# Making the Hyena filters of both layers at the start of a two-layer backbone

## The chip, the cores and the metric

The kernel runs on one core of a Trainium2 chip. The metric is the device time of one execution in microseconds (us), the median of three runs. The engines are named as the profile names them: PE (matrix products), PEld (its weight loads), DVE (vector), ACT (scalar functions), POOL (GpSimd) and SP (which issues most transfers).

## The reference, cut to what matters

Two layers work on 1,024 latent tokens and 256 context tokens of width 1,024. Each layer normalises and modulates its input by numbers made from the conditioning vectors, sends it through one input projection, and gives the parts to three mixers: latent attention, a chunkwise mLSTM and a Hyena convolution. An output projection and a convolutional FFN follow. The Hyena convolution needs a filter that depends on the layer's weights and on the position alone, not on the data:

```python
def hyena_filter(seq, w1, b1, w2, b2, w3, sin_freq):
    ...
    hdn = jnp.sin(freq * (z @ w1.astype(f32) + b1.astype(f32)))
    hdn = jnp.sin(freq * (hdn @ w2.astype(f32) + b2.astype(f32)))
    filt = hdn @ w3.astype(f32)
    ...
    h_fwd = filt[:, :HY_WIDTH] * window
    h_bwd = filt[:, HY_WIDTH:] * window
    l1 = jnp.sum(jnp.abs(h_fwd), axis=0) + jnp.sum(jnp.abs(h_bwd[1:]), axis=0)
    ...
    return taps / l1
```

Layer 0 needs it for 1,024 and for 256 positions, layer 1 for 1,024 alone.

## The kernel before, in words

Features lie on partitions and tokens along the free axis, in three blocks: two of 512 latent tokens and one of the 256 context tokens (block 2). Most float32 products are made in three passes on a high and a low part, so that one tile of a projection is many matmuls (`mm`, L252 in the trace), all into the two PSUM banks `pj` and `pk` in turn.

The program begins with the modulation numbers of layer 0 (`ada`): eight steps, each with four weight tiles by DMA, 16 matmul records into a tile `a`, an ACT copy `adarow`, four small matmuls into a tile `a`, and a DVE addition into `mods`. Between them stand the sums of squares for the first norm (`nsq` on ACT, `nacc` on DVE). From the last of these comes the scale `A`; then `norm` makes the hi/lo tiles `B` of each block with one ACT and two DVE operations for each of eight tiles.

`mixers_in` follows, for each layer: the filters, the low-rank queries (`Q0` to `Q2`, with statistics in the bank `ap`), the gate statistics of the mLSTM (`ml_gates`, bank `mm`: transposes of the gates, running sums `mlLF`/`mlLI`, maxima `mlB` and `mlast`, a recurrence `mlmrow` over nine chunks, then `mlRR`, `mldg` and `mlE`), the tiles `U0` and `U1`, the values V and the output gates O (both `by_token`, matmuls `pk<-wh,B` of 128x256), and the products with `wqk` that need the gate statistics' place in the bank `mm`.

`filters` works by blocks of positions: a matmul `f<-zemb,hw`, a `sine`, a matmul `f<-sn_h,hw`, a second `sine`, and then for every 128 positions a matmul `f<-hw,sn_h`, a window product `fb` (DVE), absolute values `fab` (ACT), sums `fl` (POOL), and the sum and difference `ft` (DVE and POOL), which go to DRAM as `taps`. A last small matmul `f<-c_ones,fl` gives the norm `hsc`. A `sine` is seven DVE operations on 64 partitions (one reads the PSUM bank, two find the multiple of two pi in `sn_k`, three subtract it in three parts, one clamps) and one ACT `Sin` into `sn_h`. The blocks follow one another through one buffer each of `sn_a`, `sn_k` and `sn_h`.

Instructions are put on each engine's queue in an order that a scheduler fixes when the program is built: `with self.later(LATER_F)` lets the filters be scheduled as if they had been written 100 instructions later, so that they fill gaps. On the chip each engine then works through its queue in that order.

Of the kernel before, what the change touches and what calls it, by code (L numbers as in the profile page):

```python
# [17 lines left out]
DEPTH = 2  # L18
# [4 lines left out]
TP = 1282                     # token axis with a zero after each stream: x 0:1024, 0, ctx 1025:1281, 0  # L23
# [11 lines left out]
# (first token, columns, stream: 0 latent / 1 context)  # L35
# [16 lines left out]
def _consts():  # L52
# [47 lines left out]
def _host(inp):  # L100
    """Lay the inputs out for the chip: slices, transposes, replication."""
# [4 lines left out]
    def colmaj(a):                       # [L, n*128] -> [L, 128, n]  # L106
        return a.reshape(a.shape[0], -1, 128).transpose(0, 2, 1)
# [52 lines left out]
    qk = np.zeros((L, 2, 2, 128, 128), np.float32)           # [L, pair, q/k, in, out]  # L160
# [9 lines left out]
    o["hyv"] = np.stack([g["hy_b1"], g["hy_b2"], g["hy_sin_freq"]], -1)   # [L,64,3]  # L170
# [19 lines left out]
class Kern:  # L190
# [52 lines left out]
    def later(self, by):  # L243
        """Scheduled as if traced `by` instructions later: work that fills gaps."""
# [9 lines left out]
    def mm3(self, out, lh, ll, rh, rl, start, stop):  # L254
        """One K tile of a float32 product carried by three float32r passes."""
# [4 lines left out]
    def ps(self, shape=(128, 512)):  # L260
        """The next of the two banks that all phases share."""
# [9 lines left out]
    def bpair(self, b):  # L271
        """hi and lo of one block of tokens; the context block carries a zero at each end."""
# [204 lines left out]
    def filters(self, L, sp, pp, tag):  # L477
# [11 lines left out]
        for blk in (range(3) if L < DEPTH - 1 else range(2)):  # L489
# [11 lines left out]
            for i in range(n // 128):  # L501
# [8 lines left out]
                if kk in (0, 8):  # L510
                    nc.vector.memset(fb[0:1, 1], 0.0)
# [1177 lines left out]
```

## Time and profile before

| | |
|---|---|
| median of three runs | 3830.62 us (3816.39 to 3831.75) |
| span of the profiled execution | 3828.4 us |
| PE busy | 3547.6 us, 93% of the span |
| DVE busy | 2001.4 us, 52% |
| ACT busy | 1294.6 us, 34% |
| POOL busy | 923.9 us, 24% |

The profile is one execution. Its span of 3828.4 us is its own time, 2.2 us under the median of the timed runs, and within their spread. "Busy" is the sum of an engine's instructions; a matmul record's end is modelled, so a busy PE is not PE at its peak. In the rows, "idle before" is the time that the engine stood still ahead of an instruction, with the instruction that ended the wait.

### The profile page before, as it was taken

What the parts mean: (1) busy time and instruction counts of PE and PEld (TensorE: products, weight loads), DVE (VectorE), ACT (ScalarE), POOL (GpSimd) and SP (SyncE); (2) the same over time, 40 slices, a digit from 0 to 9 for tenths busy, and PEclk for the clock granted to TensorE, in tenths of its full rate; (3) what the DMA queues carried; (4) which work ended last, traced back from release to release, by engine and by line L of the source; (5) the groups of instructions that cost most, each with busy time, mean ns of one, the idle gap of its engine ahead of it and who ended that gap; (6) DMA issues with size and microseconds to landing.
All of it is one profiled execution on the core that took longest, in us unless ns stands there. A gap on an engine that the chain in (4) does not pass through costs nothing.

```text
span 3828.4 us, 45926 instructions
## 1 busy us (share of the span) xinstructions
PE 3547.6 (93%) x17696; PEld 2809.5 (73%) x17696; DVE 2001.4 (52%) x3037; ACT 1294.6 (34%) x2108; POOL 923.9 (24%) x782
## 2 busy tenths in 40 slices
PE   5999869989899999999999799978999999999997
PEld 3798755556677888888888678856666778888885
DVE  5646675445565433434334765566666543444345
ACT  4433314445543221212112443324566432222222
POOL 1402442222311111111112141143334122222221
PEclk8999989989999999999999899889999999999998
DMA  5322544466242111111111222343232311111111
GB/s 176 115 69 90 198 130 141 126 168 170 71 138 66 39 34 39 39 33 34 39 39 39 94 95 88 108 141 105 54 84 80 102 44 44 45 55 45 44 50 66
DMA packets 195007, 319.46 MB, mean 83 GB/s; under 512 B 32207, under 2 KB 112160, under 8 KB 194788
## 3 DMA queue, kind: packets, MB, share of 16 engines
q1 hardware_dynamic: 194244, 316.23, 26.6%
q8 instruction: 139, 2.28, 0.3%
q14 instruction: 80, 0.66, 0.1%
q0 software_dynamic: 544, 0.31, 0.0%
HBM read 263.50 MB, written 52.81 MB: 83 GB/s over the span
## 4 chain that ended last, share of the span: by engine, by line
PE 59%; DVE 6%; DMA 3%; ACT 2%; issue 2%; POOL 1%; SPq 0%; DVEq 0%; ACTq 0%; POOLq 0%
PE u L252 29%; PE pk L252 12%; PE pj L252 12%; PE st L252 2%; PE pv L252 2%; PE hf L252 1%; ACT wh L300 1%; PE mi L252 0%; DVE B L456 0%; DMA vst<-Ph 0%; PE sm L252 0%; DVE sa L453 0%; PE mo L252 0%; DMA B<-mix 0%; DVE S L1515 0%
## 5 line engine op out<-in xcount | busy, mean ns | idle before, releaser
L252 PE MATMUL u<-B,wh 128*128 128x512 f32 (+1 forms) x3240 | 727.0, 376 | 17.6 <-ACT wh L300 10.6
L252 PEld LDWEIGHTS u<-B,wh 128*128 128x128 f32 x3240 | 573.9, 189 | 141.3 <-ACT wh L300 12.7
L301 POOL TENSOR_TENSOR wh<-wr,wh 128x1024 fp32r<-128x1024 f32 x92 | 222.3, 2416 | 1116.1 <-ACT wh L300 1116.1
L300 ACT CAST wh<-wr 128x1024 fp32r<-128x1024 f32 (+2 forms) x188 | 188.8, 1005 | 775.9 <-PE u L252 425.8
L252 PE MATMUL u<-B,wx 128*128 128x512 f32 (+1 forms) x2040 | 435.1, 367 | 2.3 <-DVE sa L1469 2.3
L252 PEld LDWEIGHTS u<-B,wx 128*128 128x128 f32 x2040 | 352.6, 189 | 70.9 <-issue 2.5
L252 PE MATMUL pj<-B,wh 128*128 128x512 f32 (+1 forms) x1644 | 381.8, 378 | 16.2 <-DVE wh L301 7.0
L252 PE MATMUL pk<-B,wh 128*128 128x512 f32 (+1 forms) x1485 | 355.9, 386 | 31.9 <-ACT S L588 7.8
L252 PEld LDWEIGHTS pj<-B,wh 128*128 128x128 f32 x1644 | 288.5, 193 | 83.6 <-issue 11.9
L252 PEld LDWEIGHTS pk<-B,wh 128*128 128x128 f32 x1485 | 265.7, 197 | 102.2 <-issue 15.3
L1515 DVE SCALAR_TENSOR_TENSOR S<-pk,mods,S 128x512 f32<-128x512 f32 (+1 forms) x220 | 152.7, 694 | 322.5 <-PE pk L252 322.3
L1344 POOL TENSOR_TENSOR Pl<-P,Ph 128x512 fp32r<-128x512 f32 (+1 forms) x168 | 219.4, 1306 | 405.9 <-ACT Ph L1343 349.1
L1515 DVE SCALAR_TENSOR_TENSOR S<-pj,mods,S 128x512 f32<-128x512 f32 (+1 forms) x220 | 152.7, 694 | 307.9 <-PE pj L252 307.8
L252 PE MATMUL st<-qh,S 96*128 96x512 f32 (+1 forms) x960 | 292.7, 411 | 15.1 <-DMA qh<-mr 7.9
L1308 DVE TENSOR_REDUCE mx<-sm 128x1 f32<-128x512 f32 (+1 forms) x400 | 227.6, 588 | 116.4 <-PE sm L252 114.1
L1468 DVE SCALAR_TENSOR_TENSOR sa<-u,ffc,sa 128x1281 f32<-128x1281 f32 (+1 forms) x88 | 124.3, 1413 | 276.3 <-ACT sa L1467 275.0
L1342 ACT ACTIVATE P<-st 128x512 f32<-128x512 f32 (+1 forms) x336 | 197.9, 590 | 162.0 <-PE st L252 82.4
L252 PE MATMUL pk<-g,wh 128*128 128x512 f32 (+1 forms) x1032 | 242.2, 370 | 7.7 <-ACT g L283 3.6
L252 PE MATMUL pj<-g,wh 128*128 128x512 f32 (+1 forms) x1032 | 245.1, 370 | 2.7 <-POOL wh L301 1.6
L252 PEld LDWEIGHTS st<-qh,S 96*128 96x128 f32 (+1 forms) x960 | 183.0, 196 | 75.0 <-DMA qh<-mr 12.2
L252 PE MATMUL pv<-Ph,B 128*64 128x512 f32 (+2 forms) x672 | 213.1, 398 | 12.7 <-ACT Ph L1343 8.4
L252 PEld LDWEIGHTS pk<-g,wh 128*128 128x128 f32 x1032 | 179.6, 189 | 43.8 <-DVE S L1515 4.2
(391 smaller groups left out, 5048.5 us busy)
## 6 DMA issues: line engine op xcount, KB each, us to landing
B<-in_adaw_dram SPq DMA_DIRECT2D x192, 256.0 KB
wr<-in_wup_dram SPq DMA_DIRECT2D x88, 512.0 KB
wr<-in_wdn_dram SPq DMA_DIRECT2D x50, 512.0 KB
wr<-in_wout_dram SPq DMA_DIRECT2D x40, 512.0 KB
wr<-in_win_dram SPq DMA_DIRECT2D x28, 512.0 KB
S<-in_xT_dram SPq DMA_DIRECT2D x16, 640.0 KB
mlrb<-rrows SPq DMA_DIRECT2D x36, 256.0 KB
B<-mix SPq DMA_DIRECT2D x32, 256.0 KB
```

The costliest lines, as they stand in the source:

```text
L252: self.nc.tensor.matmul(out, lhsT, rhs, start=start, stop=stop)
L300: self.nc.scalar.copy(hi, wr)
L301: (self.nc.gpsimd if self.wpool else self.nc.vector).tensor_tensor(lo, wr, hi, op=ALU.subtract)
L1308: nc.vector.reduce_max(st["mx"][:, qt, bi:bi + 1], ps[:, :kn], axis=AX.X)
L1342: nc.scalar.activation(P[:, :n], ps[:, :n], AF.Exp, scale=SCALE)
L1344: (nc.gpsimd if j % 2 else nc.vector).tensor_tensor(Pl[:, :n], P[:, :n], Ph[:, :n], op=ALU.subtract)
L1468: nc.vector.scalar_tensor_tensor(y[:, 1:W], pu[:, 0:W - 1], cw[:, 0:1], y[:, 1:W], op0=ALU.mult, op1=ALU.add)
L1515: nc.vector.scalar_tensor_tensor(x, ps, self.mods[L][:, 40 + m, s:s + 1], x, op0=ALU.mult, op1=ALU.add)
```

## The change

Both layers' filters are made by one call of `filters` at the very beginning of the program, written ahead of the modulation steps, in place of one call in each layer's `mixers_in`. Inside, the loop over blocks of positions is outermost and each block is made for layer 0 and then for layer 1, so that the transfers of the position features `zemb` and of the windows `win` serve both. Layer 1's sines do three of their steps (the two of `sn_k` and the clamp) on POOL instead of DVE. The input transfers of the filters go from SP's queue to POOL's. The tags are doubled in `rf`, and the PSUM pool of the modulation gives two of its six banks to `f0`. In `mixers_in` the pool `pf` keeps the bank `ap` alone.

```diff
-    def sine(self, ps, n, freq, b, sp):
+    def sine(self, ps, n, freq, b, sp, eng):
...
-        nc.vector.tensor_scalar(k[:, :n], a[:, :n], 1.0 / (2.0 * math.pi), magic, op0=ALU.mult, op1=ALU.add)
-        nc.vector.tensor_scalar(k[:, :n], k[:, :n], -magic, None, op0=ALU.add)
+        eng.tensor_scalar(k[:, :n], a[:, :n], 1.0 / (2.0 * math.pi), magic, op0=ALU.mult, op1=ALU.add)
+        eng.tensor_scalar(k[:, :n], k[:, :n], -magic, None, op0=ALU.add)
...
-    def filters(self, L, sp, pp, tag):
+    def filters(self, sp, pp, tag):
...
+        for L in range(DEPTH):
...
+            nc.gpsimd.dma_start(w1, a["hw1"][L])
...
-        for blk in (range(3) if L < DEPTH - 1 else range(2)):
+        for blk in range(3):
...
+            layers = range(DEPTH) if isx else range(DEPTH - 1)
...
+            for L in layers:
+                w1, w2, w3, hv = W[L]
+                e = (nc.vector, nc.gpsimd)[L]
...
+                h = self.sine(ps[:64, :n], n, hv[:, 2:3], hv[:, 0:1], sp, e)
...
+                nc.gpsimd.dma_start(win, a["hwin"][:, kk])
+                for L in layers:
...
             fp = self.pool(e, f"pf{L}", PSUM, f0=2, ap=1)
-            with ExitStack() as e1, self.later(LATER_F):
...
-                self.filters(L, rp, fp, "f0")
...
-                pp = self.pool(e0, "p0", PSUM, a0=6)
+                rf = self.pool(e0, "rf", hw1=2, hw2=2, hw3=2, hv=2, fb=2, fab=2, ft=2, win=2, zemb=1)
+                pp = self.pool(e0, "p0", PSUM, a0=4, f0=2)
+                self.hsc = [self.t(self.cp, [128, 2, 2], f"c_hsc{L}") for L in range(DEPTH)]
+                with self.later(LATER_F):
+                    self.filters(rf, pp, "f0")
```

The program's order on the engines moves with it at three places. The rows are engine queues as they are built: output, inputs, shape of the output, and a count where one row stands for several.

On PE, just ahead of the first input projection (`pk` from a tile `B`), the queue of before has the last modulation step and one filter matmul:

```order
L365 MATMUL a_74_378<-B_379,c_cs_184 32x256 x2
L252 MATMUL a_80_397<-c_sel_187,adarow_395 128x2 x2
L252 MATMUL f_213_733<-zemb_731,hw_208_723 64x512
L252 MATMUL pk_990<-B_445,wh_980 128x512
```

In the queue of after, filter matmuls stand between the modulation steps (here behind the second and the fifth of eight, and behind the last). `sn_hv` is a sine made for layer 0, `sn_hg` one made for layer 1 with POOL:

```order
L365 MATMUL a_176_657<-B_658,c_cs_184 32x256 x2
L252 MATMUL f_40_253<-sn_hv_251,hw_28_223 64x512
L252 MATMUL f_44_266<-zemb_238,hw_31_230 64x512
L252 MATMUL a_182_676<-c_sel_187,adarow_674 128x2 x2
...
L252 MATMUL f_48_279<-sn_hg_277,hw_32_231 64x512
L252 MATMUL f_53_294<-hw_29_224,sn_hv_264 128x512
L252 MATMUL a_203_745<-c_sel_187,adarow_743 128x2 x2
...
L252 MATMUL a_224_814<-c_sel_187,adarow_812 128x2 x2
L252 MATMUL f_58_307<-hw_33_232,sn_hg_290 128x512
L252 MATMUL f_64_322<-hw_29_224,sn_hv_264 128x512
L252 MATMUL pk_1154<-B_862,wh_1144 128x512
```

Of the 31 rows of filter matmuls that the program of after has, 7 now stand ahead of the first projection, and 24 still stand among layer 0's projections; before, 1 of layer 0's 18 stood ahead of it and 17 behind, and layer 1's 13 stood in its own `mixers_in`.

On ACT, in the stretch of the modulation steps, the queue of before has no table load after the one that precedes the first `rs_s`. In after `Sin` and square root take turns between the copies `adarow`, with five more loads ahead of the first `B`:

```order
L473 ACT_TABLE_LOAD
L473 ACTIVATE sn_hv_251<-sn_av_242 64x512
L434 ACTIVATE nsq_927<-S_178 128x512
L368 COPY adarow_674<-a_176_657 128x256
...
L414 ACT_TABLE_LOAD
L414 ACTIVATE rs_s_940<-rs_v_938 128x8
...
L473 ACT_TABLE_LOAD
L473 ACTIVATE sn_hg_277<-sn_ag_268 64x512
```

On PE in layer 0, the gate statistics stand elsewhere between the V and O products. Before, 258 rows lie between the gates' transposes and the first product with `wqk`, and the steps of the chain are spread among them; its last steps read:

```order
L252 MATMUL mm_1562<-mldg_1563,c_ones_191 128x128
L252 MATMUL pk_2280<-wh_2270,B_445 128x256
...
L252 MATMUL mm_1562<-mldg_1566,c_ones_191 128x128
L252 MATMUL pj_2308<-wh_2270,B_445 128x256
...
L252 MATMUL mm_2067<-wqk_1593,S_1683 128x128
```

In after, 35 rows of V stand between the transposes and the running sums, 48 rows of O between these and `mlast`, and then the rest of the chain follows without a row between:

```order
L252 MATMUL pj_2472<-wh_2440,B_905 128x256
L252 MATMUL mm_1687<-c_ident_189,mlast_1682 1x128 x2
L252 MATMUL mm_1713<-c_ones_191,mlmrow_1692 128x2
L785 MATMUL mm_1721<-c_ident_189,mlRR_1659 128x128 x3
L252 MATMUL mm_1726<-mldg_1727,c_ones_191 128x128
L252 MATMUL mm_1726<-mldg_1730,c_ones_191 128x128
L252 MATMUL mm_2231<-wqk_1757,S_1847 128x128
```

All filter matmuls stand ahead of this place in both programs: it is PE row 753 before and 766 after, 13 rows later. The transposes moved from row 495 to row 672. The queues that are left, in layer 1 and behind it, differ by small exchanges of neighbours only.

## Rows read from the trace of the kernel before

**Rows 1.** Busy time by stretches: PE, PEld, DVE, ACT, POOL, then granted clock, DMA.
```profile
20.00:58.90 38.90, 29.09 (x188) 16.76 (x188) 17.02 (x47) 17.57 (x36) 0.81 (x16) 0.93 0.84 270
58.90:94.00 35.10, 24.89 (x77) 18.04 (x78) 34.29 (x60) 18.69 (x32) 1.38 (x1) 0.74 0.06 17
94.00:110.40 16.40, 16.40 (x80) 11.14 (x79) 6.80 (x10) 5.27 (x10) 7.81 (x9) 1.00 0.22 70
```

**Rows 2.** PE's timeline at the start: start, duration, instruction, records, idle before.
```profile
28.13 1.94 PE L365 MATMUL a<-B,c_cs 128*32 128x256 f32 x16 [5.74 <-DMA B<-in_adaw_dram]
...
55.33 0.61 PE L252 MATMUL a<-c_sel,adarow 128*128 128x2 f32 x4 [0.57 <-ACT adarow L368]
...
58.95 0.80 PE L252 MATMUL pk<-B,wh 128*128 128x512 f32 x1 [2.02 <-ACT B L455]
```

**Rows 3.** Filter matmuls (tile f) on PE by stretches: length, busy time, records.
```profile
0.00:58.90 58.90, 1.07 (x2) 0.95 0.83 276
58.90:110.40 51.50, 6.36 (x12) 0.82 0.11 34
110.40:230.00 119.60, 10.02 (x26) 0.97 0.31 104
2150.00:2310.00 160.00, 13.32 (x28) 0.94 0.25 82
```

**Rows 4.** DVE operations that write or read sn_a, by stretches.
```profile
58.90:94.00 35.10, 7.31 (x12) 0.74 0.06 17
...
2150.00:2310.00 160.00, 18.70 (x24) 0.94 0.25 82
```

**Rows 5.** PE's waits from 58 to 230 us: total, times, longest.
```profile
PE f L252 <- ACT sn_h L472: 7.7, 2, 4.0
```

**Rows 6.** PE's waits from 2174 to 2310 us (layer 1).
```profile
PE f L252 <- ACT sn_h L472: 2.5, 1, 2.5
PE mm L252 <- DVE mlE L792: 1.1, 1, 1.1
PE mm L252 <- DVE mldg L783: 0.7, 1, 0.7
PE pj L252 <- DVE mltmp L764: 0.7, 1, 0.7
PE mm L252 <- DVE mlTT L779: 0.7, 1, 0.7
```

**Rows 7.** PE's timeline around the wait for a sine in layer 1.
```profile
2244.03 1.16 PE L252 MATMUL f<-sn_h,hw 64*64 64x512 f32 x2 [2.52 <-ACT sn_h L472]
2245.13 4.96 PE L252 MATMUL pk<-B,wh 128*128 128x512 f32 x14
2249.92 2.26 PE L252 MATMUL pj<-B,wh 128*128 128x512 f32 x9
```

**Rows 8.** Timeline of ACT around the first sine of layer 0.
```profile
77.34 1.28 ACT L472 ACT_TABLE_LOAD   x1
78.64 0.63 ACT L472 ACTIVATE sn_h<-sn_a 64x512 f32<-64x512 f32 x1
```

**Rows 9.** Groups by line: durations in ns, least, median, greatest.
```profile
L508 DVE TENSOR_TENSOR fb<-f,win x18: 616/686/692, 98.8 to 2270.1; 128x512 f32<-128x512 f32 x18
...
L521 DVE TENSOR_TENSOR ft<-fb x18: 404/576/959, 100.3 to 2275.5; 128x256 f32<-128x256 f32 x18
...
L963 POOL TENSOR_SCALAR S<-S,c_hyd x4: 2846/3188/3804, 454.4 to 2522.0; 128x1280 f32<-128x1280 f32 x2, 128x1024 f32<-128x1024 f32 x2
```

**Rows 10.** PE's timeline in layer 0: the gates' transposes and the first wqk.
```profile
192.35 0.85 PE L713 MATMUL mm<-c_ident,S 16*128 16x16 f32 x11
...
227.20 0.60 PE L252 MATMUL mm<-wqk,S 128*128 128x128 f32 x4
```

**Rows 11.** Timeline of the gate chain in layer 1, PE and DVE.
```profile
2279.69 0.39 DVE L716 COPY mlG<-mm 128x80 f32<-128x80 f32 x2 [0.49 <-PE mm L713]
...
2282.38 0.24 DVE L726 SCALAR_TENSOR_TENSOR mlLF<-mlG,mle 128x80 f32<-128x80 f32 x1 [2.07 <-ACT mle L721]
...
2285.02 0.42 DVE L738 COPY mlRR<-mm 128x256 f32<-128x256 f32 x1 [2.39 <-PE mm L252]
...
2291.73 0.60 PE L252 MATMUL mm<-c_ident,mlast 128*1 128x128 f32 x4
...
2292.37 0.41 DVE L759 COPY mlrow<-mm 1x256 f32<-1x256 f32 x1 [1.64 <-PE mm L252]
2292.82 0.15 DVE L764 TENSOR_TENSOR mltmp<-mlmrow,mlrow 1x8 f32<-1x8 f32 x1
...
2302.08 0.38 PE L252 MATMUL mm<-c_ones,mlmrow 1*128 1x2 f32 x2
...
2306.91 1.22 PE L252 MATMUL mm<-wqk,S 128*128 128x128 f32 x4 [1.10 <-DVE mlE L792]
```

**Rows 12.** PE's groups from 188.9 to 227.2 us: the V and O products.
```profile
L252 PE MATMUL pj<-wh,B 128*128 128x256 f32 x139 | 18.5, 284 | 0.0
```

More of the change, by code (lines that the diff above doesn't have):

```diff
@@ L348, in load_consts2 @@
                 nc.gpsimd.dma_start(d[nm], a[nm][L])
-            d["hsc"] = self.t(cp, [128, 2, 2], f"c_hsc{L}")
+            d["hsc"] = self.hsc[L]
             self.lc.append(d)
@@ L475 @@
     two_pi = (6.28125, 0.0019350051879882812, 3.019916e-07)
-    def filters(self, L, sp, pp, tag):
+    def filters(self, sp, pp, tag):
         nc, a = self.nc, self.a
-        w1 = self.t(sp, [33, 64], "hw1")
-        w2 = self.t(sp, [64, 64], "hw2")
-        w3 = self.t(sp, [64, 512], "hw3")
-        hv = self.t(sp, [64, 3], "hv")
-        nc.sync.dma_start(w1, a["hw1"][L])
-        nc.sync.dma_start(w2, a["hw2"][L])
-        nc.sync.dma_start(w3, a["hw3"][L])
-        nc.sync.dma_start(hv, a["hyv"][L])
-        for blk in (range(3) if L < DEPTH - 1 else range(2)):
+        W = []
+        for L in range(DEPTH):
+            w1 = self.t(sp, [33, 64], "hw1")
+            w2 = self.t(sp, [64, 64], "hw2")
+            w3 = self.t(sp, [64, 512], "hw3")
+            hv = self.t(sp, [64, 3], "hv")
+            nc.gpsimd.dma_start(w1, a["hw1"][L])
+            nc.gpsimd.dma_start(w2, a["hw2"][L])
+            nc.gpsimd.dma_start(w3, a["hw3"][L])
+            nc.gpsimd.dma_start(hv, a["hyv"][L])
+            W.append((w1, w2, w3, hv))
+        l1 = [None] * DEPTH
+        for blk in range(3):
             n = 512 if blk < 2 else 256
@@ L492, in filters @@
             isx = blk < 2
+            layers = range(DEPTH) if isx else range(DEPTH - 1)
             z = self.t(sp, [33, 512], "zemb")
-            nc.sync.dma_start(z[:, :n], a["zemb"][:, c0:c0 + n])
-            ps = self.t(pp, [128, 512], tag)
-            self.mm(ps[:64, :n], w1, z[:, :n])
-            h = self.sine(ps[:64, :n], n, hv[:, 2:3], hv[:, 0:1], sp)
-            ps = self.t(pp, [128, 512], tag)
-            self.mm(ps[:64, :n], w2, h[:, :n])
-            h = self.sine(ps[:64, :n], n, hv[:, 2:3], hv[:, 1:2], sp)
+            nc.gpsimd.dma_start(z[:, :n], a["zemb"][:, c0:c0 + n])
+            hs = []
+            for L in layers:
+                w1, w2, w3, hv = W[L]
+                e = (nc.vector, nc.gpsimd)[L]
+                ps = self.t(pp, [128, 512], tag)
+                self.mm(ps[:64, :n], w1, z[:, :n])
+                h = self.sine(ps[:64, :n], n, hv[:, 2:3], hv[:, 0:1], sp, e)
+                ps = self.t(pp, [128, 512], tag)
+                self.mm(ps[:64, :n], w2, h[:, :n])
+                hs.append(self.sine(ps[:64, :n], n, hv[:, 2:3], hv[:, 1:2], sp, e))
             for i in range(n // 128):
@@ L521, in filters @@
-                nc.vector.tensor_tensor(ft[:, 0], fb[:, 0], fb[:, 1], op=ALU.add)
-                f, r = (1, 0) if kk in (6, 7) else (0, 1)
-                nc.gpsimd.tensor_tensor(ft[:, 1], fb[:, f], fb[:, r], op=ALU.subtract)
-                nc.sync.dma_start(self.taps[L, kk] if isx else self.tapsc[kk - 8], ft.rearrange("p a b -> p (a b)"))
-            if blk in (1, 2):
+                nc.gpsimd.dma_start(win, a["hwin"][:, kk])
+                for L in layers:
+                    ps = self.t(pp, [128, 512], tag)
+                    self.mm(ps, hs[L][:, 128 * i:128 * i + 128], W[L][2])
+                    fb = self.t(sp, [128, 2, 256], "fb")
+                    nc.vector.tensor_tensor(fb, ps.rearrange("p (a b) -> p a b", a=2),
+                                            win.unsqueeze(1).to_broadcast([128, 2, 256]), op=ALU.mult)
+                    if kk in (0, 8):
+                        nc.vector.memset(fb[0:1, 1], 0.0)
+                    ab = self.t(sp, [128, 2, 256], "fab")
+                    nc.scalar.activation(ab, fb, AF.Abs)
+                    if kk in (0, 8):
+                        l1[L] = self.t(sp, [128, 256], f"fl1{L}")
+                        nc.gpsimd.tensor_tensor(l1[L], ab[:, 0], ab[:, 1], op=ALU.add)
+                    else:
+                        nc.gpsimd.tensor_tensor(l1[L], l1[L], ab[:, 0], op=ALU.add)
+                        nc.gpsimd.tensor_tensor(l1[L], l1[L], ab[:, 1], op=ALU.add)
+                    ft = self.t(sp, [128, 2, 256], "ft")
+                    nc.vector.tensor_tensor(ft[:, 0], fb[:, 0], fb[:, 1], op=ALU.add)
+                    f, r = (1, 0) if kk in (6, 7) else (0, 1)
+                    nc.gpsimd.tensor_tensor(ft[:, 1], fb[:, f], fb[:, r], op=ALU.subtract)
+                    nc.sync.dma_start(self.taps[L, kk] if isx else self.tapsc[kk - 8], ft.rearrange("p a b -> p (a b)"))
@@ L526, in filters @@
+            for L in layers if blk in (1, 2) else ():
                 ps = self.t(pp, [128, 512], tag)
                 for ct in range(2):
-                    self.mm(ps[:, 2 * ct:2 * ct + 2], l1[:, 128 * ct:128 * ct + 128], self.ones[:, 0:2])
+                    self.mm(ps[:, 2 * ct:2 * ct + 2], l1[L][:, 128 * ct:128 * ct + 128], self.ones[:, 0:2])
                 st = blk - 1
@@ L534, in filters @@
                 nc.vector.reciprocal(v, v)
-                nc.vector.tensor_copy(self.lc[L]["hsc"][:, st], v[:, :, 0])
+                nc.vector.tensor_copy(self.hsc[L][:, st], v[:, :, 0])
     def project(self, L, tiles, blocks):
@@ L623, in mixers_in @@
         with ExitStack() as e:
-            fp = self.pool(e, f"pf{L}", PSUM, f0=2, ap=1)
-            with ExitStack() as e1, self.later(LATER_F):
-                rp = self.pool(e1, f"rf{L}", sn_a=1, sn_k=1, sn_h=1, hw1=1, hw2=1, hw3=1, hv=1, fb=2, fab=1, ft=1,
-                               fl1=1, fls=1, win=2, zemb=1)
-                self.filters(L, rp, fp, "f0")
+            fp = self.pool(e, f"pf{L}", PSUM, ap=1)
             with ExitStack() as e1:
```

26 lines of the change are left out of this document (5 added, 21 removed).

## The prediction
> **What bounds the kernel now.** PE is busy 93% of the span, so a stretch is worth reading only where PE stands idle or does work that the change moves. I read the stretches of the table of busy times first, then PE's waits in the two `mixers_in`, then the timelines behind the largest of these. Three things come out. From 20 to 58.9 us PE is busy 29.1 of 38.9 us: the modulation steps follow one another on PE from 28.1 us on, with waits of about half a microsecond, and the end of that chain sets the first projection at 58.95 [rows 1, 2]. From 58.9 to 94 us the norm bounds: DVE is busy 34.3 of 35.1 us, PE 24.9, at a mean granted clock of 0.74; then PE works off 16.4 us without a gap, so that Q0 and Q1 are done at 110.4 [rows 1]. From there on PE is the bound, and what counts is its own work and its waits for the end of a chain on other engines: two waits for a sine in layer 0, 7.7 us [rows 5], and in layer 1 one of 2.5 us and four of the gate chain, 3.2 us [rows 6].
>
> **Layer 1, what is removed.** Its filter matmuls are 13.32 us of PE in a stretch where PE is the bound [rows 3]. The wait for a sine, 2.5 us, goes with them [rows 6], and so does the slow stretch behind it: 14 records took 4.96 us, where the next 9 took 2.26, or 0.25 each, which makes 3.5 for 14; 1.5 us [rows 7]. The gate statistics start earlier in the queue there, so I count their four waits as gone, 3.2 us [rows 6]. DVE loses 18.7 us of sine work and more [rows 4], but it is not the bound there: worth nothing by itself. Sum **-20.5**; bounds -13.3 (the matmuls alone, if the waits only change their name) and -23.
>
> **Layer 0, what is added.** In both programs all filter matmuls stand ahead of the first `wqk` product, which is 13 rows later than before, and these 13 are layer 1's. So that product, at 227.2 us before [rows 10], moves by 13.3 us of PE work [rows 3] plus whatever PE's idle time changes by. That change has four parts.
>
> *The start.* Seven filter rows instead of one stand ahead of the first projection. At 6.36/6 = 1.06 us a row [rows 3], the first falls into the 5.7 us in which PE waits for weights [rows 2], two stand behind the last step, where there was a gap of 2 us and one row already, and four, 4.2 us, lie between the steps. PE is in order: the second row waits for a whole sine (seven DVE steps among the sums of squares), the fourth for one that goes from DVE to POOL, back, and to POOL again. Before, two waits for a sine were 7.7 us together [rows 5]; here the modulation steps between the rows give the sines time, so I take half, 3.8. Four table loads stand ahead of copies `adarow`, on which the next small matmuls wait; at 1.28 us [rows 8] that is 5.1, of which I take half, 2.6, since each step gives ACT some slack. Together 10.6: the first projection is **10 later, near 69 us** (bounds 4, with the matmuls alone, and 17, with all waits). Six rows of this, 6.4 us, are matmuls already in the 13.3; idle grows by 3.6.
> The Trainium skill ("ScalarE: Activation LUTs", *What ACT_TABLE_LOAD costs*) puts a switch of sets at about 2.66 us, 1.28 for the load and 1.38 of drain, and advises to batch calls by set, which speaks against this change; by it the 2.6 would be 5.3 and the sum 2.7 more. The trace does not show the drain: the load starts at 77.34 and ends at 78.62, and the ACTIVATE follows at 78.64 [rows 8], so I go by the row.
>
> *The norm.* Two sines lay among its DVE operations: 7.31 us and two steps of 0.4 outside these rows, 8.1 [rows 4]. Now it is one sine (4.1), seven `fb` at 0.69 and seven `ft` at 0.58 [rows 9], 13.0. DVE bounds that stretch, so the norm ends 4.9 later again, but PE also gets 2 us more of filter work there, and it had 10.2 us idle in which to do it [rows 1]. I take the change of idle as 0 (bounds -4 and +5).
>
> *The waits for sines behind it.* One of 4.0 us was there from 110 us on [rows 5]; now more sines end there and POOL makes three steps of some. POOL's nearest row is 3.19 us for 1,024 to 1,280 columns [rows 9], about 1.4 for 512, three times DVE's 0.4, so a layer 1 sine comes some 3 us later. DVE has room and PE has other rows to do; I take 1 us more (bounds -4 and +20).
>
> *The gate chain.* Before, 258 rows of PE lay over it. In after each link must be covered by what stands between. From the copy `mlG` to `mlLF` it takes 2.9 us in layer 1 [rows 11]; 35 V rows at 18.5/139 = 0.133 [rows 12] give 4.7: covered. From the copy `mlRR` to `mlast` on PE it is 6.7 [rows 11], 48 O rows give 6.4: covered but for little. Behind `mlast` nothing stands: the copy `mlrow`, 0.4, and 18 steps of 0.19 by the start of the copy and of the first step on, 3.8 to 4, are PE's to wait; measured in layer 1, among other DVE work, it was 9.7 to the next PE row [rows 11]. From there to `wqk` it is 4.8 us, of which PE works 1.9 [rows 11], assuming 0.5 for each of its groups: 2.9 more. Together about 7.5 (bounds 7 and 13), and 1 us of slow clock behind such a wait, as in layer 1 [rows 7].
>
> Sum for layer 0: 13.3 + 3.6 + 0 + 1 + 8.5 = **+26.4**. What moves from SP's queue to POOL's (21 transfers, each issued in the order of POOL's work) I cost at nothing: the first weights are needed after 20 us, when POOL is nearly idle, 0.8 of 38.9 us busy [rows 1]; without that cover the context block's clearing on POOL, which stands behind them, would be late and with it the third block's projections: that is inside the bound of +5 for the norm.
>
> **The sum.** -20.5 + 26.4 = +5.9, so a span of 3834.3 against 3828.4; the median stands 2.2 above that span, so I predict a median of about 3835 (3836.5 by the sum; I round toward no change since the norm's idle may well shrink). A difference of less than 0.5%, 19 us, is about what a measurement of this kernel cannot tell from none.
>
> **The rivals.**
> *Faster: the start hides it.* PE idles 9.8 us until 58.9 and 10.2 in the norm [rows 1], 20 together, more than the 13.3 of added matmuls. If the filter rows fall into these, and if DVE gets through the recurrence `mlmrow` before PE has worked off the O rows, layer 0 loses about 2, and the whole gains 18 to 19: 3811. For it: the idle time is there. Against it: half of it waits for weights or for the end of the very chain that the filters are queued in, and only one of the seven rows stands ahead of the first modulation step. It decides if the first projection starts before about 61 us and the gate waits stay under 2. Chance 0.15.
> *Slower: every sine stalls PE.* Ten sines now serve one in-order PE in one stretch, four with three hand-overs between DVE and POOL. If six of them make PE wait 3.8 us each, as the two before did [rows 5], that is 23 against the 8.8 that I have counted (3.8, 4.0 and 1): 14 more, net +20, a median of 3851; if nine do, 3862. It decides from waits for `sn_hv` and `sn_hg` of some 22 us in the first 260 us on. For it: both waits before were of this size although the scheduler had placed the rows. Against it: after the norm PE has 100 us of other work to put between. Chance 0.22.
> *The change does not do what it says.* 24 of 31 filter rows still stand among layer 0's projections, so it is no pass at the beginning. That is in the forecast; where these rows fill no gaps, layer 0 pays their full 13.3, as I counted.
>
> **How the numbers follow.** Forecast, within 0.5%: chance 0.63, its own range 3818 to 3849 (layer 1 from -13 to -23, layer 0 from +17 to +37, seldom both at their ends). With the two rivals the range that leaves out 2 in 10 is 3809 to 3857. Faster by over 0.5% 0.15, within 0.63, slower 0.22.
>
> **What would show it.** Filter matmuls in layer 1's stretch gone, and `wqk` to the end of layer 1's `mixers_in` shorter by about 20; the first projection near 69 us (under 64: the start was costed too high); Q0 and Q1 done near 120 to 124; in layer 0 a wait of PE for `mlmrow` and one for `mlE`, 7 to 8 us together, behind 48 O rows; the first `wqk` near 254 us against 227. I am wrong if the waits for sines exceed 22 us, if the gate wait is missing, or if the time between the first `wqk` of layer 0 and layer 1's start, which I take as unchanged, moves by more than 5 us.

## The result, and the profile after

The changed kernel takes 3851.62 us (median of 4 runs, 3846.36 to 3856.78) where the kernel before takes 3827.56 (4 runs, 3816.39 to 3831.75): a ratio of 1.0071, 95% interval 1.0052 to 1.0089, 24 us more by these medians and 27 by the ratio. Its profiled execution has a span of 3855.0 us, 26.6 over that of before. The filters left layer 1 as forecast; layer 0 paid more than layer 1 gave back.

The start times of the same PE rows in the two profiles say where (the last row of layer 0's FFN stands for the end of layer 0):

| PE row | before, us | after, us | shift |
|---|---|---|---|
| first input projection | 58.95 | 73.69 | +14.7 |
| first `wqk`, layer 0 | 227.2 | 267.2 | +40.0 |
| first row of layer 0's Hyena (`hf`) | 444.0 | 486.4 | +42.4 |
| last `u<-B,wx` of layer 0 | 2068.4 | 2120.3 | +51.9 |
| first `wqk`, layer 1 | 2306.9 | 2335.6 | +28.7 |
| first row of layer 1's Hyena (`hf`) | 2509.2 | 2531.9 | +22.7 |
| end of the span | 3828.4 | 3855.0 | +26.6 |

Layer 0 loses 40.0 us up to its first `wqk` and 11.9 behind it; layer 1 gains 23.2 from the end of layer 0 to its own `wqk`, and 29.2 up to its first `hf`; the last stretch loses 3.9 again. For layer 1 the `hf` row is the fairer mark: its first `wqk` has 288 rows of V and O (`pj` and `pk` from `wh,B`, 128x256) ahead of it before and 240 after, so 48 rows, about 6.4 us at 0.133 each [rows 12], only moved to the other side of it. The queues of layer 1 therefore differ by more than small exchanges of neighbours.

Both profiles hold the same 17,696 PE records, and PE is busy 17.6 us longer and idle 9.0 us longer in after. Two stretches, from layer 0's `hf` to its last `u<-B,wx` and from there to layer 1's `hf`, read (length, then PE's busy time first), before and then after:

```profile
444.00:2068.40 1624.40, 1514.17 (x7741) 1196.14 (x7740) 778.10 (x1116) 502.42 (x799) 365.22 (x275) 0.96 0.28 84
2068.40:2509.17 440.77, 400.68 (x2236) 330.08 (x2235) 272.64 (x480) 166.17 (x288) 99.78 (x123) 0.93 0.28 92
```
```profile
486.40:2120.30 1633.90, 1526.65 (x7741) 1203.79 (x7740) 777.58 (x1116) 502.86 (x799) 364.09 (x275) 0.96 0.28 83
2120.30:2531.87 411.57, 375.04 (x2208) 317.53 (x2207) 237.98 (x431) 152.31 (x271) 72.61 (x99) 0.95 0.28 90
```

In the first of them the same 7,741 records, none of which the change touches, take 12.5 us more of PE's busy time. The second has 28 records fewer and 25.6 us less busy time.

The filter matmuls of after by stretches, where [rows 3] had them before:

```profile
0.00:58.90 58.90, 9.60 (x10) 1.00 0.84 271
58.90:110.40 51.50, 12.35 (x16) 0.89 0.20 71
110.40:230.00 119.60, 16.34 (x42) 0.93 0.17 59
```

These are the same 68 records as before in layer 0 and layer 1 together, but 38.3 us of busy time instead of 30.8. The reader sees why in PE's timeline of after, where a filter row (two records) in the start takes 1.9 to 2.1 us instead of 1.06:

```profile
36.22 1.96 PE L252 MATMUL f<-sn_hv,hw 64*64 64x512 f32 x2 [0.64 <-ACT sn_hv L473]
37.98 1.91 PE L252 MATMUL f<-zemb,hw 33*64 33x512 f32 x2
...
55.49 2.07 PE L252 MATMUL f<-hw,sn_hv 64*128 64x512 f32 x2
...
129.08 3.02 PE L252 MATMUL pj<-B,wh 128*128 128x256 f32 x24
...
261.72 0.55 PE L252 MATMUL mm<-c_ones,mlmrow 1*128 1x2 f32 x2 [3.99 <-DVE mlmrow L772]
```

The last but one is the end of Q0 and Q1: 132 us, against 110.4 [rows 1]. PE's waits in the first 260 us of after (what is waited for, total, times, longest), against [rows 5]:

```profile
PE pk L252 <- ACT S L599: 12.2, 1, 12.2
PE pk L252 <- ACT S L682: 5.2, 1, 5.2
...
PE f L252 <- ACT sn_hg L473: 0.7, 1, 0.7
PE f L252 <- ACT sn_hv L473: 0.6, 1, 0.6
```

The sines hardly make PE wait any more: 1.3 us instead of 7.7. In their place stands one wait of 12.2 us at the end of the norm (4.5 before), where the bank of a finished projection is copied by ACT behind the norm's own ACT steps, and one of 5.2 for the copies of V. The gate chain adds waits for `mlmrow` (4.0 us), `mlast` (1.4), `mlE` (1.1), `mlTT` (0.7) and `mldg` (0.4), 7.6 us together, none of which layer 0 had before.

The stretches of after that answer to [rows 1] (busy time of PE, PEld, DVE, ACT, POOL, then granted clock, DMA): the modulation, the norm, and layer 1 from its first projection to its first `wqk`.

```profile
22.30:73.69 51.39, 44.81 (x200) 21.34 (x200) 33.54 (x76) 27.97 (x48) 9.58 (x11) 1.00 0.64 211
73.69:110.30 36.61, 23.82 (x62) 13.06 (x61) 35.99 (x50) 14.97 (x25) 24.64 (x40) 0.84 0.18 65
2202.33:2335.60 133.27, 119.28 (x673) 101.86 (x674) 75.55 (x151) 54.77 (x94) 22.09 (x51) 0.94 0.22 71
```

In the norm POOL is now busy 24.6 us, where it had 1.4 in the 35 us of before [rows 1], and the norm's own DVE steps have become slower (groups of after by line: busy time, mean ns):

```profile
L453 DVE SCALAR_TENSOR_TENSOR ntmp<-S,A,nrb 128x512 f32<-128x512 f32 x16 | 16.6, 1068 | 0.0
L456 DVE SCALAR_TENSOR_TENSOR B<-ntmp,mods,B 128x512 fp32r<-128x512 f32 x16 | 13.4, 855 | 0.0
L519 DVE TENSOR_TENSOR fb<-f,win 128x512 f32<-128x512 f32 x7 | 4.8, 683 | 0.6 <-POOL ft L534 0.6
...
L534 POOL TENSOR_TENSOR ft<-fb 128x256 f32<-128x256 f32 x7 | 11.8, 1695 | 9.3 <-DVE fb L519 7.3 <-DVE fb L522 2.0
```

The same two norm steps before:

```profile
L456 DVE SCALAR_TENSOR_TENSOR B<-ntmp,mods,B 128x512 fp32r<-128x512 f32 x16 | 11.3, 738 | 0.0
L453 DVE SCALAR_TENSOR_TENSOR ntmp<-S,A,nrb 128x512 f32<-128x512 f32 x16 | 11.2, 740 | 0.0
```

That is 7.5 us more for 32 instructions that the change does not touch.

### The profile page after: what moved, and what is told of

It is laid out like the page before. It is cut to its first block, busy times and chain, and to the rows that moved or that the text cites. A ratio compares the mean times of both kernels' runs of the same rounds, so it can differ in the third digit from the quotient of the medians.

```text
span 3855.0 us, 45894 instructions
## 1 busy us (share of the span) xinstructions
PE 3565.2 (92%) x17696; PEld 2815.5 (73%) x17696; DVE 1994.4 (52%) x3025; ACT 1295.7 (34%) x2109; POOL 938.0 (24%) x815
## 5 line engine op out<-in xcount | busy, mean ns | idle before, releaser
L252 PE MATMUL u<-B,wh 128*128 128x512 f32 (+1 forms) x3240 | 730.3, 377 | 18.9 <-ACT wh L300 10.6
L252 PEld LDWEIGHTS pj<-B,wh 128*128 128x128 f32 x1644 | 288.7, 193 | 90.8 <-issue 14.7
L252 PE MATMUL st<-qh,S 96*128 96x512 f32 (+1 forms) x960 | 294.5, 413 | 18.3 <-DMA qh<-mr 13.9
L252 PE MATMUL pv<-Ph,B 128*64 128x512 f32 (+2 forms) x672 | 216.5, 403 | 10.6 <-ACT Ph L1350 7.1
```

Of the source, the lines that this page charges most:

```text
L252: self.nc.tensor.matmul(out, lhsT, rhs, start=start, stop=stop)
```

## The experiments

The theory of places: layer 0's loss is a sum of separate things at separate places (a late start, a slow norm, the copies of V, a bare gate chain), and each can be undone alone. Its rival, moved work: layer 0 pays what layer 1 saves, wherever the filters stand in it. A third theory, contention, says that POOL's filter steps slow the norm's DVE steps. The table holds what the texts below draw on: the ratio to the kernel before with its interval, and from the profile, in us, the start of the first projection, PE's wait for the copy at the norm's end, the start of the first `wqk`, and layer 1 (from layer 0's last `u<-B,wx` to layer 1's `wqk`).

| kernel | ratio (95%) | first proj. | norm's end | `wqk` | layer 1 |
|---|---|---|---|---|---|
| before | 1 | 59.0 | 4.5 | 227.2 | 238.5 |
| after | 1.0071 (1.0052 to 1.0089) | 73.7 | 12.2 | 267.2 | 215.3 |
| e5 change again | 1.0064 (1.0047 to 1.0080) | 71.2 | 12.0 | 263.8 | 214.8 |
| e1 own banks | 0.9994 (0.9980 to 1.0008) | 69.4 | 12.0 | 248.9 | 214.4 |
| e11 own banks again | 0.9996 (0.9987 to 1.0005) | 69.6 | 11.6 | 248.7 | 214.5 |
| e2 one pass, old place | 1.0025 (1.0010 to 1.0041) | 65.3 | 7.1 | 257.8 | 211.7 |
| e3 layer 0 only at start | 1.0031 (1.0020 to 1.0042) | 74.7 | 5.7 | 223.7 | 246.9 |
| e6 inputs first | 1.0088 (1.0073 to 1.0103) | 85.7 | 5.6 | 273.1 | 214.9 |
| e7 clearing on DVE | 1.0061 (1.0046 to 1.0076) | 70.8 | 11.4 | 262.6 | 215.3 |
| e10 banks, DVE sines | 1.0005 (0.9997 to 1.0014) | 81.5 | 8.6 | 254.6 | 214.4 |
| e12 banks, `ft` on DVE | 1.0000 (0.9989 to 1.0012) | 74.2 | 10.6 | 248.8 | 211.8 |
| e4 layer 1 in attention | 1.0214 (1.0197 to 1.0231) | 61.0 | 4.1 | 230.3 | 214.2 |
| e9 the same, later | 1.0075 (1.0060 to 1.0090) | 61.5 | 4.3 | 231.1 | 215.0 |

**e1, banks of their own for the filters.**

The filters use two `ms` banks of the pool that layer 0's mixers use later, and the modulation has three banks instead of four.

```diff
-            pp = self.pool(e, f"pm{L}", PSUM, mm=1, ms=2)
+            pp = self.pm0 if L == 0 else self.pool(e, f"pm{L}", PSUM, mm=1, ms=2)
...
+            epm = ExitStack()
+            self.pm0 = self.pool(epm, "pm0", PSUM, mm=1, ms=2)
...
-                pp = self.pool(e0, "p0", PSUM, a0=4, f0=2)
+                pp = self.pool(e0, "p0", PSUM, a0=3)
...
-                    self.filters(rf, pp, "f0")
+                    self.filters(rf, self.pm0, "ms")
```

> The changed kernel, but the filters' two PSUM banks are taken from a pool that is open before the modulation and stays open through layer 0's mixers, so that the banks of the low-rank norm and of the gates do not wait for the last filter matmul (modulation keeps three banks instead of four). In its queue the gate chain of layer 0 is spread among V and O products again, but for its last two steps. By the theory of places (layer 0's loss is the sum of a late start, a slow norm, and two exposed chains) PE's gate waits of 7.5 us in layer 0 shrink to about 2 and the time falls by 5 to 6 us, to about 3846. By the rival of moved work (layer 0 pays the matmuls of layer 1, wherever they stand) nothing changes: 3852.

Measured 3820.89 us, the time of before (3824.12 in that session). The expected gate waits shrank to 1.9 us (`mlE` 1.1, `mldg` 0.8), but the wait for V's copies went too, and the granted clock stayed up. From 112 us to the first `wqk`, first after, then this kernel:

```profile
112.00:267.20 155.20, 140.33 (x783) 113.24 (x782) 89.66 (x165) 55.93 (x91) 56.84 (x73) 0.93 0.23 82
```
```profile
112.00:248.90 136.90, 133.32 (x773) 107.34 (x771) 92.18 (x156) 52.56 (x87) 57.53 (x73) 0.99 0.28 92
```

PE's idle time falls from 14.9 to 3.6 us, and nearly the same records take 7.0 us less at a granted clock of 0.99 instead of 0.93. So the `wqk` is 18.3 us earlier, three times what I had given the edit, and the rival of moved work falls with it: the moved matmuls are all still there.

The rows show what the banks do. In after, the bank `ap` of Q's statistics and the gates' transposes into `mm` are first written when the last filter matmul (`f<-c_ones,fl`) has been done; with banks of their own for the filters, both come long before it (`ms<-c_ones,fl` here):

```profile
218.82 0.50 PE L252 MATMUL f<-c_ones,fl 128*128 128x2 f32 x4
221.63 2.29 PE L252 MATMUL ap<-c_ones,S 128*128 128x2 f32 x20
241.56 1.40 PE L720 MATMUL mm<-c_ident,S 16*128 16x16 f32 x20
```
```profile
144.95 0.95 PE L252 MATMUL ap<-c_ones,S 128*128 128x2 f32 x8
176.51 0.91 PE L720 MATMUL mm<-c_ident,S 16*128 16x16 f32 x12
219.74 0.50 PE L252 MATMUL ms<-c_ones,fl 128*128 128x2 f32 x4
```

**e11, the same again** beside two others, and **e5, the changed kernel again.**

> The first experiment once more, on the same chip as the two others. It gained 31 us over the changed kernel where the theory of places gave 6: in its profile 18 us up to layer 0's first wqk and 17 behind it, most of these in layer 0's attention. If the part behind is a difference between executions, the time is 12 to 20 below the changed kernel (3836 to 3844 where before is 3830); if the banks do it, it equals before again, within 0.15%.

> The changed kernel once more, beside the next two on the same chip. In its first profile 12 us of the 52 by which layer 1 began late arose behind layer 0's gate chain, in stretches that the change does not touch. By the theory of places these 12 are a difference between executions and the loss up to the first wqk (40 us) comes back within 2: the time lies 22 to 27 above before. By the rival that the change also slows the later stretches, both come back.

Both repeat: e11 at 0.9996 equals before again, e5 at 1.0064 is slower again. The `wqk` stands at 263.8 and 248.7, 15 us apart. From there to layer 0's last `u<-B,wx` before takes 1841.2 us, after 1853.1, e5 1850.2, e1 1836.5 and e11 1846.8, and no single wait there carries the difference. So of the 17 us that e1's profile gained behind the `wqk`, 10 did not come again in e11, the same kernel. From `hf` to the last `u<-B,wx` the same 7,741 records keep PE busy 1526.7 us in after, 1522.6 in e5, 1516.0 in e1 and 1517.8 in e11: 5 to 11 us of the difference is PE taking longer over the same rows, and what makes it do so is left open. So 15 to 18 of the 25 to 31 us between the changed kernel's medians and those with banks of their own are shown at their place.

**e2, one pass at the old place.** The filters of both layers in layer 0's mixers, with the banks of e1.

```diff
-                with self.later(LATER_F):
-                    self.filters(rf, pp, "f0")
...
+            here = ((0, 1), ())[L]
...
+            if here:
+                with ExitStack() as e1, self.later(LATER_F):
+                    rp = self.pool(e1, f"rf{L}", hw1=2, hw2=2, hw3=2, hv=2, fb=2, fab=2, ft=2, win=2, zemb=1)
+                    self.filters(rp, *((self.pm0, "ms") if L == 0 else (fp, "f0")), here)
```

> The changed kernel's single pass for both layers, but written in layer 0's mixers instead of ahead of the modulation, with the banks of the run before; sines of layer 1 with POOL, inputs through POOL's queue as in the change. By the theory of places the first projection is back at 59 to 60 us (15 earlier), layer 1 keeps its gain of 23 us, the norm keeps part of its slowness and the gate chain stays exposed in its queue (7.5 us): 3836 to 3840. By the rival of moved work the start does not matter: 3850 to 3852.

Measured 3832.59 us where before is 3824.12: 8.5 us above it, inside the 8 to 12 expected. The first projection is at 65.3, not 59 to 60, since three filter rows still stand ahead of it; the wait at the norm's end is 7.1; the bare gate chain, `mlmrow` 4.0 us first of all, is back. Against e1, which has the same banks, the first projection is 4.1 us earlier and the norm's end 4.9 shorter, and still the `wqk` is 8.9 later and the kernel 11.7 us slower. So with banks of their own the early place costs about 4 us at the start and 5 at the norm's end and gives back more behind them: banks alone do not cover the gate chain, nor, as after shows, does the early place alone when both layers' filters stand there.

**e3, layer 0 alone at the start**, layer 1's filters in its own mixers.

```diff
-                    self.filters(rf, pp, "f0")
+                    self.filters(rf, pp, "f0", (0,))
```

> Only layer 0's filters are made at the start (sines on DVE alone); layer 1's are made in its own mixers as before. By the theory of places the first projection is late by 10 to 13 us with seven filter rows ahead of it, the gate chain is covered in its queue, layer 1 gains nothing: about 12 to 16 us above before, 3840 to 3844. By the rival of moved work nothing has been moved into layer 0: the time of before, 3828, within 4.

Measured 1.0031, 10 to 12 us, and `wqk` at 223.7: the start is 15.7 us late, and layer 0 catches nearly all of it up, since its filters are done early and its chain is covered. (At the `wqk` 48 rows of O, some 6.4 us, stand behind it that stood ahead before; at the first `hf` the kernel is 1.4 us late.) A late first projection by itself is not lost. The loss is in layer 1 here (246.9 us against 238.5), with the filters where they were, but not as they were: three steps of each sine are still done on POOL there, their inputs come by POOL's queue, and the buffers are doubled. The last filter row comes at 2285.3 instead of 2275.2, PE waits 4.0 us for `mlmrow` and 3.1 for V's copies. Which of the three makes the filters late was not tried. I had expected the right size for the wrong reason.

**e4 and e9, layer 1's filters in layer 0's attention**, where PE idles 54 of 510 us before; e9 begins them only when the modulation steps for later, which use the same bank `pk`, are issued.

The first fence is e4's edit, the second e9's.

```diff
                     with self.later(LATER_A):
+                        for _ in range(2):
+                            if L == 0:
+                                next(self.fg, None)
```
```diff
                     with self.later(LATER_A):
+                        for _ in range(4):
+                            if L == 0 and not todo:
+                                next(self.fg, None)
```

> Layer 0's filters in its mixers as before; layer 1's are made in layer 0's attention, two matmul steps at a time between the key tiles, through the bank pk that the modulation steps use there, with three steps of each sine on POOL. PE idles 54 of 510 us in that stretch of before and DVE 250. By the theory of places layer 1 gains its 23 us and attention pays 0 to 10: 3806 to 3818. By the rival of moved work attention pays at least 13.3, plus waits: 3818 to 3825.

> As the fourth experiment (layer 0's filters in its mixers as before, layer 1's in layer 0's attention through the bank pk), but the filter steps begin only when the 40 modulation steps that share this bank are issued, four to a key-tile round. In the fourth experiment 30 of the 40 steps stood in 200 us at a granted clock of 0.65. By the theory that the filters' sines held that bank and crowded the modulation steps together, attention returns to 508 to 525 us, layer 1 keeps its gain of 23, and the time is 3815 to 3825 where before is 3830: faster by 0.2 to 0.4%. By the rival that sines between the key tiles are dear in themselves (table loads between exponentials, POOL beside DVE), attention stays over 560 us and the kernel is slower than before.

Both expectations failed. e4 takes 81 us more than before. Layer 1 keeps its gain (214.2), but attention grows by over 100 us: the modulation steps behind the filters' share of `pk` are crowded into a stretch of 200 us in which PE is busy 70 us in a hundred at a granted clock of 0.65, and its largest wait is for the modulation weights' transfers (25.9 us in 21 waits):

```profile
750.00:850.00 100.00, 70.26 (x339) 34.37 (x338) 19.63 (x41) 22.57 (x42) 20.55 (x21) 0.65 0.47 145
850.00:950.00 100.00, 70.97 (x322) 38.54 (x321) 30.24 (x63) 20.05 (x43) 17.15 (x21) 0.64 0.49 145
```

e9 takes that cause away, and the rest stays: the filters now stand in the last 136 us of attention, where the nearest stretch of before took 99 (first before from its last modulation step, then e9; the two do not hold quite the same records):

```profile
980.40:1079.60 99.20, 90.36 (x387) 64.47 (x387) 55.75 (x97) 54.74 (x108) 33.57 (x27) 0.97 0.25 72
```
```profile
987.40:1123.50 136.10, 113.91 (x367) 64.61 (x367) 88.14 (x127) 69.41 (x127) 69.87 (x70) 0.81 0.32 90
```

PE's busy time grows by 23.6 us although the filter rows are 13.3 us of work at the price of before [rows 3] (many take 2.07 us here, so about 20), at a granted clock of 0.81 instead of 0.97, and its idle time by 13. The whole of attention, from its first modulation step on, goes from 512.7 to 549.9 us. The idle time of a stretch was not free to be filled: 13.3 us of matmuls with their sines cost 37 there.

**e6, inputs first.** The banks of e1, and positions and the filters' smaller weights (`hw1`, `hyv`, `hw2`) on SP's queue ahead of the tokens.

```diff
+            self.filters_load(rf)
             xs = []
             for k in range(8):
                 x = self.row()
                 nc.sync.dma_start(x[:, :T], a["xT"][k])
```

> The changed kernel with the banks of the first experiment, and the small inputs of the filters (positions, first and second weights) loaded on SP's queue ahead of the latent tokens. In its queue the filters' first rows stand ahead of the first sum of squares, and 15 rows ahead of the first projection. By the theory of places PE and DVE use their idle time until 22 us for the first two sines, but twice as many rows stand in the modulation's chain: first projection at 70 to 80, norm shorter by the fb and ft that are already done; time 3812 to 3822. By the rival that DVE's contention with POOL makes the norm slow, taking filter work out of the norm should give 7 us more: 3805 to 3815, with the mean of the norm's first DVE step back at 0.74 us.

Measured 1.0088, slower than the change. Fifteen rows now stand ahead of the first projection, all but three of them later than 17 us, and PE waits for their sines (PE's waits, first 130 us):

```profile
PE ms L252 <- ACT sn_hv L473: 9.9, 3, 7.9
...
PE ms L252 <- ACT sn_hg L473: 8.8, 2, 5.1
```

The longest of these waits, 7.9 us, ends at 12.8 us, when PE has nothing else to do, and costs nothing; the others make 10.8. The first projection falls back to 85.7. The norm's first step has a mean of 0.76 us, since POOL has done most of its work by then: the contention is nearly gone and the wait at the norm's end is 5.6, but the start costs more than that saves.

**e7, the ones of V set on DVE.**

```diff
-                    nc.gpsimd.memset(v[:, :, :, 64:65], 1.0)
+                    nc.vector.memset(v[:, :, :, 64:65], 1.0)
```

> The changed kernel with one edit: the column of ones of the values V is set on DVE instead of POOL, where it stands behind the context filter's sums. By the theory of places the wait of PE for the copy of V, 5.2 us, shrinks to under 1 and the time falls by 4 to 5: about 3847. By the rival that this wait is only the first of several that end at the same time (the copy also waits for ACT's own filter work), it falls by less than 2.

The wait stays, 4.7 us, and the ratio too (1.0061). The rival was right: POOL only came last. The profile now names DVE's setting of the ones as what the copy waits for, and that stands behind the filters' last `ft` on DVE (it ends at 210.01), so the edit changed the queue and not the wait. ACT was idle for 2.2 us ahead of the copy, so at most 2.2 of the 4.7 hang on the setting.

**e8, POOL beside the norm of before.** The kernel before with 16 additions on POOL.

```diff
+            if self.probe and b < 2:
+                jk = self.t(self.probe, [128, 256], "junk")
+                nc.gpsimd.tensor_tensor(jk, tmp[:, 0:256], tmp[:, 256:512], op=ALU.add)
```

> The kernel before with one addition: for each of the 16 tiles of the first norm's two latent blocks, POOL adds the two halves of the norm's intermediate tile into a spare tile (128x256). Nothing reads it. By the theory of contention the norm's first DVE step (0.74 us before) rises to a mean of 0.9 to 1.1 while POOL runs and the first norm takes 4 to 8 us longer; by the rival that the norm of the changed kernel is slow only for its added DVE operations, the mean stays at 0.74 and the norm keeps its length within 1 us.

```profile
L459 DVE SCALAR_TENSOR_TENSOR B<-ntmp,mods,B 128x512 fp32r<-128x512 f32 x16 | 14.2, 913 | 0.0
L453 DVE SCALAR_TENSOR_TENSOR ntmp<-S,A,nrb 128x512 f32<-128x512 f32 x16 | 14.1, 918 | 0.6 <-POOL junk L457 0.6
...
L457 POOL TENSOR_TENSOR junk<-ntmp 128x256 f32<-128x256 f32 x16 | 24.2, 1540 | 51.3 <-DVE ntmp L453 51.3
```

DVE's steps go from 0.74 to 0.92 us with nothing changed but POOL's work, 5.8 us in 32 steps; `wqk` is 5.4 later, and the one run takes 3841.9 us (before, in that session, 3828.76 to 3837.48). Contention is shown as a mechanism.

**e10 and e12, what POOL does beside the norm**: with the banks of e1, all sines on DVE (e10), or POOL's half of `ft` on DVE (e12).

```diff
-                    nc.gpsimd.tensor_tensor(ft[:, 1], fb[:, f], fb[:, r], op=ALU.subtract)
+                    nc.vector.tensor_tensor(ft[:, 1], fb[:, f], fb[:, r], op=ALU.subtract)
```

> The changed kernel with the banks of the first experiment and all sines on DVE alone. In its queue the whole gate chain stands among V products (its last step 37 rows ahead of wqk), and eight filter rows stand ahead of the first projection. By the theory that POOL work beside the norm is what makes its DVE steps slow, little changes there, since POOL keeps the differences and sums: mean of the first norm step 0.9 to 1.1, and the first projection is 2 to 4 us later than with POOL's sines, the gate waits gone: 3818 to 3828, within 0.3% of the first experiment. By the rival that the split of the sines is what crowds POOL and DVE, the norm's mean falls under 0.85 and the time is 8 us below the first experiment.

> The first experiment (filters' banks in a pool of their own) with one more edit: POOL's half of ft, the difference of the two directions, is made on DVE; POOL keeps the sums fl. In the norm of the first experiment POOL worked 25 us beside DVE, about half of it on these differences, and the norm's first DVE step had a mean of 1.07 us. The queue keeps the gate chain where it was. By the theory that POOL's reads beside DVE make the norm slow, the mean falls to 0.85 to 0.95; the seven added DVE steps cost 4 us and the shorter ones give back 3 to 5, so the time stays within 3 us of the first experiment, 0.998 to 1.0005 of before. By the rival that it is the filters' own DVE work that delays the norm, the mean stays over 1.0 and the time grows by 4 us or more.

e10 is level with before (1.0005): the first projection 12 us later than in e1 instead of 2 to 4, the norm's first step at 0.84 us, and the two nearly cancel. In e12 that step falls to 0.77 us, below what I had expected, and the time stays where it was (1.0000), `wqk` at 248.8. The norm's second step stays at 0.86 us, though, and the first projection, 74.2, is 4.7 us later than in e1. So contention is real, and taking part of it away did not change the time; that DVE's own steps then take the room that POOL's contention took is my reading, not shown.

## Why the prediction came out as it did

The time lies inside the range, 3809 to 3857, but in the case that I gave 0.22, not in the likeliest one. The steps, with the first profile's measure and that of e5 in brackets where it differs (the rows for layer 0 up to `wqk` make 34.8 of its 40.0):

| step | predicted | measured |
|---|---|---|
| layer 1, to its `wqk` | -20.5 | -23.2 (-23.7) |
| layer 1, to its `hf` | not listed | -29.2 (-28.1) |
| first projection | +10 | +14.7 (+12.3) |
| more filter matmuls in layer 0 | +13.3 | +20.8 |
| norm's end, change of idle | 0 | +7.7 (+7.5) |
| waits for sines, first 260 us | +4.8 | -6.4 |
| copies of V | not listed | +5.2 |
| gate waits in layer 0 | +7.5 | +7.6 |
| PE's busy time up to the first `wqk` | +13.3 | +28.0 |
| PE's idle time up to the first `wqk` | +13.1 | +12.0 |
| up to the first `wqk` | +26.4 | +40.0 (+36.6) |
| from there to layer 1 | 0 | +11.9 (+9.0) |

**Right:** the gate chain, link by link: the wait for `mlmrow` came to 4.0 us behind the 48 O rows, those for `mlE` and its neighbours to 3.6.

**Right as a sum, by luck in the parts:** layer 1's gain and layer 0's idle time. In layer 1 the matmuls and the wait for a sine went, but the four gate waits, 3.2 us, did not; two others of 3.6 took their place:

```profile
PE mm L252 <- DVE mlLF L733: 1.9, 1, 1.9
PE mm L252 <- DVE mlmrow L772: 1.7, 1, 1.7
```

What made up for them are the 48 rows that moved behind the `wqk`. Up to `hf` PE's busy time fell by 25.6 us where 14.8 were forecast (13.3 and 1.5) and its idle time by 3.6 where 5.7 were; the granted clock rose from 0.93 to 0.95 there. In layer 0 the idle time came near the forecast because a wait at the norm's end (+7.7) and one for V (+5.2) met sines that waited less (-6.4).

**The step that failed:** "moves by 13.3 us of PE work plus whatever PE's idle time changes by". PE's busy time up to the first `wqk` rose by 28.0 us. The filter matmuls themselves make 20.8 of it; 7.2 lie in other rows, with the granted clock of after at 0.93 from 112 us on where e1 has 0.99. By its own sign, that the time between the first `wqk` of layer 0 and layer 1's start moves by no more than 5 us, the prediction is wrong too: it moved by 11.9 (9.0 in e5). That sign is weak, since e1 and e11, one kernel, differ by 10.3 there.

**Wrong in size:** the filter rows of the start. I priced them at 1.06 us, the row of a stretch in which PE runs on; between the modulation steps of after they take 1.9 to 2.1. [rows 2] could only warn of this: its 1.94 us at 28.13 is a modulation step of 16 records, not a filter row. Before, six such steps take 1.85 to 1.94 us and two 1.07, and the one filter row of the start takes 1.07; after, all eight steps take 1.93 to 1.94. The price goes with the stretch and is not the same in each execution: in e11 two of the seven rows took 1.07 and 1.12, among modulation steps of 1.07 (before, then e11):

```profile
47.95 1.07 PE L365 MATMUL a<-B,c_cs 128*32 128x256 f32 x16
55.86 1.07 PE L252 MATMUL f<-zemb,hw 33*64 33x512 f32 x2
```
```profile
54.29 1.12 PE L252 MATMUL ms<-hw,sn_hv 64*128 64x512 f32 x2
55.88 1.07 PE L365 MATMUL a<-B,c_cs 128*32 128x256 f32 x16
65.89 2.07 PE L252 MATMUL ms<-hw,sn_hg 64*128 64x512 f32 x2
```

At 2 us, four rows between the steps cost 8 and the start comes to 14, near the 14.7 measured, though in part by luck: the sines made PE wait 1.4 us there instead of the 3.8 counted, and the two rows that were put into a gap and behind the last step cost 4.

**Wrong as a step:** "I take the change of idle as 0" in the norm. I counted the filters' DVE instructions but let the norm's own keep their price. They rose by 7.5 us, with POOL beside them. PE's idle time there rose by 7.7, beyond the bound of +5: the end of the norm is waited for in a bank's copy behind ACT's norm steps, 12.2 us. Still, e10 and e12 take part of the contention away and do not get the time back.

**Missed:** the copies of V, and the lower granted clock of the stretch with these waits (0.93). That both go when the filters have banks of their own (e1) shows what the change really brought in: layer 0's later pools wait behind the last filter. The order of rows showed the gate chain bare; I took that as given and did not ask what had pushed it there.

**The slower rival** gave nearly the right time (3851) for the wrong reason. It rested on PE waiting 22 us for sines, and the profile has 1.3. Its mechanism appears only in e6. **The faster rival** is refuted by the first projection at 73.7, not under 61.

## What to carry to other kernels

Price a moved instruction by the rows of the stretch that it moves into, and those of its new neighbours too: the same filter row cost 1.06 us in the projections and mostly 1.9 to 2.1 among the modulation steps, and 32 untouched DVE steps cost 7.5 us more with POOL at work beside them. When a block is pulled forward, ask which buffers its last instruction now holds and what is written into them next: here banks of their own brought the early place from 0.7% slower back to the time of the kernel before, and no further. Idle time in a busy stretch is not room: 13.3 us of matmuls with long chains cost 37 us in attention's idle time.

## What the runs showed of the hardware that was not expected

DVE and POOL slow each other. A DVE step that reads two SBUF tiles went from 0.740 to 0.918 us with POOL additions beside it whose result nothing reads (e8) and to 1.068 in the changed kernel, and POOL's own `ft` took a mean of 1.70 in the norm, against 0.96 over all of before; the DVE step `fb`, which reads a PSUM bank and one SBUF tile, kept its 0.68 (0.69 in [rows 9]). The Trainium skill ("SBUF — State Buffer", *SBUF: two separate sides*) says that DVE, with two SBUF inputs, and POOL take an exclusive lock on a shared pair of ports for a whole instruction and the other blocks; the trace agrees in which steps are slowed.

The granted clock as the profile gives it did not always go with the price of a row. In e11 it did: it reads 0.50, the lower of the two levels (1.2 and 2.4 GHz), from 38 to 50 us, where modulation steps take 1.93 us, and 1.00 from 54 to 62, where they take 1.07. In after it reads 1.00 from 22 to 74 us, although all eight steps take 1.93 to 1.94 and the filter rows there 1.9 to 2.1. So the price of the start is read from the rows themselves.

Two of POOL's three sine steps on 64x512 took 0.61 to 1.53 us, with a median of 0.70, half of the 1.4 that the prediction drew from a larger form; the third, one operation in place on `sn_k`, took 1.49 to 1.81, with a median of 1.52.
